# Lending one PSUM bank of the block products to the small products beside them

## The chip, the cores and the metric

The kernel runs on one core of a Trainium2 chip. The metric is the time of one execution on the device in microseconds, as the median of the runs. One execution is profiled, and the profile's "span" is the time from its first to its last recorded instruction. Engines are named as the profile names them: PE (matrix multiplies), PEld (its weight loads), DVE, ACT, POOL, and SP, which only issues transfers here.

## What is computed

One inference step of one layer, for 1024 prompt rows and for 8 samples of 4 rows, all with 1024 channels. After a normalisation the rows are multiplied by `w_in`, whose columns feed two branches and the gates:

```python
def layer(x, c, C0, n0, m0, k_past, v_past, ...):
    h, gate = adaln_in(x, c, w_ada, b_ada, g_norm)
    mq, mk, mv, mi, mf, mo, mz, aq, ak, av, az, gm, ga = split_in(h @ w_in)
    y_m, C, n, m = mlstm_branch(mq, mk, mv, mi, mf, mo, mz, C0, n0, m0, b_i, b_f, g_mn)
    ...
    o = attn_prompt(q, k, v, sinks)
    ...
    y_a = o.astype(x.dtype) * jax.nn.silu(az)
    u = jax.nn.sigmoid(gm) * (y_m @ w_mo) + jax.nn.sigmoid(ga) * (y_a @ w_ao)
    x = x + gate * (u @ w_o)
```

The mLSTM branch has 4 heads with a matrix memory that is carried over chunks of 128 rows. The attention branch has 8 query heads on 2 key heads, sees a window of 128 rows, and has a sink term in its softmax. Everything is float32. At the end stands another normalisation, and the memories, keys and values are outputs too.

## The kernel before

**Big products.** The large multiplications with `w_in` go in pairs of 128-column jobs over all 1024 prompt rows: 20 pairs, of the kinds `head_in` (6, the inputs of the mLSTM heads), `gate` (8), `query_gate` (2, the attention's output gate) and `head_gate` (4). `block_products` (L1511) does each pair by a scheme with 7 products instead of 8, numbered 1 to 7. Each is 12 matmuls of 128x512, since every operand is split into a high and a low part and three of the four combinations are summed. Sums and differences of blocks are formed beforehand, partly on DVE, partly by copying one product's bank into the next one's, from which it goes on accumulating. From the second pair on, the order is 5, 6, 2, 7, then product 1 of the next pair, then 3, 4. In the first pair product 5 stands ahead of 3.

**PSUM.** There are 8 banks, two for each of the tags g, a, b and o (L197 to 207). Product 1 takes a bank of g (`bx`, called X), which goes on into product 2; W (`bw`, from g) is a copy of X and goes into products 3 and 6. Tag a holds product 5 (`bz`, called Z, L1550) and Y (`by`, L1563), which starts as a copy of W and goes into products 7 and 4. Product 5 is copied out to SBUF by ACT, right behind the product in the program:

```python
                elif i == 5:
                    p5 = ht([128, 512], "p5")
                    S.copy(p5, Z)
```

The bank is not used again until product 5 of the next pair. Small products share the two b banks and the two o banks.

**Small products** come from generators in streams: attention units `unit(g, b0)` (L836, 16 of them; the text calls them unit (3,4) and the like), mLSTM heads `head(h)` (L1027), `sample_head(h)` (L1147), the sample rows of each pair (`smp`, L1360, and `smpo`, L1372) and others. At each `yield lag, banks` a generator says when its next visit is due and which banks that takes. In a unit the visits are: scores `sc` into one o and one b bank, which DVE reads together with the mask (the profile's `CUSTOM_DVE_ANT_0 p<-sc,cst,sink`) for the maximum; exponentials on ACT, and the load of V rows from `vdD` over the queries in `uqv`; the division; the transposes `pt` into a b bank; `oT`, the product with V, into a b bank.

**The planner.** `Side` (L115) decides at build time where small products go. It has a clock, `side.now`, that each matmul moves on by its estimated time, and `tick` is called after every third matmul of a big product. A visit is put in when it is due and its banks are free by the planner's account: a bank counts as taken for 3.5 us (b) or 5.5 us (o) after each use.

```python
HOLD = {"b": 3.5, "o": 5.5}
...
    def fits(self, banks):
        return all(sorted(self.free[b])[banks.count(b) - 1] <= self.now for b in set(banks) & set(HOLD))
```

PE's order is thereby fixed in the program. On DVE, ACT and SP a scheduler of the framework orders the instructions, and what a buffer or bank has to wait for is put in as semaphores. A PE instruction whose bank isn't free yet holds up all of PE behind it. A transfer that SP issues waits on SP for what it overwrites, and holds up the transfers behind it.

**Stages beside each other.** Units run first, beside pairs 1 to 7. Heads start when units are done (`side.held`): head 0 loads its inputs (`hq`, `hk`, `hkn`, `hv`, the exponents `et`, the weights `qw`) with six transfers on SP, and its first steps on DVE are `MEMSET hv`, `et<-et,cst` and `qw<-qw,hq`. Sample heads come among the later heads. When the last big product is done, everything left in the streams is put in, and then the output products `g_w_ao`, `g_w_mo` and the last product with `w_out` follow (banks `foX`, `foW`, `foZ`, `foY`).

Of the kernel before, what the change touches and what calls it, by code (L numbers as in the profile page):

```python
# [10 lines left out]
F32 = mybir.dt.float32  # L11
# [98 lines left out]
HOLD = {"b": 3.5, "o": 5.5}  # L110


class Side:
# [4 lines left out]
    def __init__(self, each, limits, quiet, patience):  # L118
        self.each, self.patience, self.free = each, patience, {b: [0.0, 0.0] for b in HOLD}
        self.now, self.last, self.quiet, self.products = 0.0, 0.0, quiet, 0  # L120
        self.held = {}
        self.streams = {n: {"max": m, "gap": g, "wait": [], "live": [], "next": 0.0} for n, (m, g) in limits.items()}

    def add(self, stream, gen, banks=""):
# [16 lines left out]
    def tick(self, joined=False):  # L141
        self.each()
        for name, st in self.streams.items():
            held = name in self.held and self.held[name]()
            if st["wait"] and not held and len(st["live"]) < st["max"] and self.now >= st["next"]:
                self.begin(st)
        ripe = sorted((i for st in self.streams.values() for i in st["live"] if self.now >= i[1]), key=lambda i: i[1])
        for item in [i for i in ripe if not i[2]]:
            self.step(item)
        ripe = [i for i in ripe if i[2] and self.now >= i[1]]  # L150
        able = [i for i in ripe if self.fits(i[2])]
        late = [i for i in able if self.now >= i[1] + self.patience]
        if not joined and (self.now < self.last + self.quiet or (len(able) < 2 and not late)):
            return
        kept = set()
        for item in sorted(ripe, key=lambda i: "r" in i[2] or -("t" in i[2])):
            if not self.fits(item[2]) or kept & set(item[2]):
                if self.now >= item[1] + self.patience:
                    kept |= set(item[2])
                continue  # L160
            self.take(item[2])
            self.step(item)
            self.last = self.now

    def fits(self, banks):
        return all(sorted(self.free[b])[banks.count(b) - 1] <= self.now for b in set(banks) & set(HOLD))

    def take(self, banks):
        for b in (b for b in banks if b in HOLD):
            self.free[b].remove(min(self.free[b]))  # L170
            self.free[b].append(self.now + HOLD[b])

    def until(self, done):
        while not done():
# [14 lines left out]
def body(tc, a):  # L189
    nc = tc.nc  # L190
    with ExitStack() as ctx:
        cp = ctx.enter_context(tc.tile_pool(name="cp", bufs=1))
        sp = ctx.enter_context(tc.tile_pool(name="sp", bufs=1))
        ps = ctx.enter_context(tc.tile_pool(name="ps", bufs=1, space=PSUM))
        dp = ctx.enter_context(tc.tile_pool(name="dp", bufs=1, space=DRAM))

        def pg(shape, name):  # L197
            return ps.tile(shape, F32, tag="g", bufs=2, name=name)

        def pa(shape, name):  # L200
            return ps.tile(shape, F32, tag="a", bufs=2, name=name)

        def pb(shape, name):
            return ps.tile(shape, F32, tag="b", bufs=2, name=name)

        def po(shape, name):
# [78 lines left out]
            free.append(ins)  # L285

        side = Side(stores, {"m": (2, 35.0), "a": (5, 7.0), "x": (2, 0.0), "s": (2, 20.0), "g": (1, 0.0), "e": (2, 0.0)}, 2.0, 4.0)
        def mm(out, lhsT, rhs, start, stop, share=1, more=False):
            n = int(np.prod(rhs.shape[1:]))
            side.now += max(n, 250) / 2400 if rhs.dtype == F32R else max(n * 4 // share, 128) / 2400  # L290
            side.products += 1
            in_order(nc.tensor.matmul(out, lhsT, rhs, start=start, stop=stop, skip_group_check=more))  # L292
# [171 lines left out]

        def x_rows(p, dg):
            n = PARTS[p][1]
            rows = (pa, pa, pg)[p]([128, 512], f"xb{p}")[:, :n]
            for c in range(0, n, 128):
                m = min(128, n - c)
                mm(rows[:, c:c + m], one[:m], dg[:m, c:c + m], start=True, stop=True)  # L470
            return rows
# [59 lines left out]
        banks = [pg]  # L531
# [979 lines left out]
        def block_products(jobs, hook):  # L1511
            flat = [(0, 1)]
            for n in range(len(jobs)):
                nx = [(n + 1, 1)] if n + 1 < len(jobs) else []
                flat += [(n, i) for i in (5, 6, 2, 7)] + nx if n else [(n, 6), (n, 2), (n, 7)] + nx + [(n, 5)]
                flat += [(n, 3), (n, 4)]

            def split_ahead(j):
                if j < len(flat):
                    jobs[flat[j][0]].split(flat[j][1])  # L1520

            bank = lambda pool, name: pool([128, 512], name)
            jobs[0].load()
            yield
            jobs[0].samples()
            split_ahead(0)
            jobs[0].first_sums()
            split_ahead(1)
            yield

            def filled(pool, name, src, n):
                b = bank(pool, name)
                if n == 0:
                    mm(b, wh[:, 0], blocks["b11"][0][0], start=True, stop=True)
                S.copy(b, src)
                return b

            X, W, Y, Z, NX = None, None, None, None, None
            for j, (n, i) in enumerate(flat):
                job_ = jobs[n]  # L1540
                nxt = jobs[n + 1] if n + 1 < len(jobs) else None
                hook(n, i)
                job_.kind.ahead(job_, i)
                if i == (5 if n else 1) and nxt:
                    nxt.load()
                split_ahead(j + 2)
                if i == 1:
                    o = NX = bank(pg, "bx")
                elif i == 5:
                    o = Z = bank(pa, "bz")  # L1550
                else:
                    o = {2: X, 3: W, 4: Y, 6: W, 7: Y}[i]
                new = i in (1, 5)
                wh, wl = job_.w.pop(i)
                for k in range(4):
                    bh, bl = blocks[OPERANDS[i]][k]
                    mm(o, wh[:, k], bh, start=(new and k == 0), stop=False, more=not new)
                    mm(o, wh[:, k], bl, start=False, stop=False, more=not new)
                    mm(o, wl[:, k], bh, start=False, stop=(k == 3), more=not new)
                    if k < 3:  # L1560
                        side.tick()
                if i == 6:
                    Y = filled(pa, "by", W, n)  # L1563
                elif i == 2:
                    job_.done(0, 0, X)
                elif i == 5:
                    p5 = ht([128, 512], "p5")
                    S.copy(p5, Z)
                elif i == 3:
                    job_.done(0, 1, p5, W)  # L1570
                elif i == 4:
                    job_.done(1, 0, Y)
                if i == (7 if n else 5):
                    job_.done(1, 1, p5, Y)
                if i == (2 if n else 7) and nxt:
                    nxt.samples()
                    nxt.first_sums()
                if j == 0 or (i == 3 and nxt):
                    X = NX
                    W = filled(pg, "bw", X, j)  # L1580
                side.tick()
# [46 lines left out]
        def first_split(n, i, eng):  # L1628
# [16 lines left out]
        rows = {p: x_rows(p, dgs[p]) for p in (0, 2)}  # L1645
# [12 lines left out]
        rows[1] = x_rows(1, dgs[1])  # L1658
        acc = [(pg([128, 384], "g_ak0"), po([128, 384], "g_av0")),
               (po([128, 384], "g_ak1"), pg([128, 384], "g_av1")),  # L1660
               (pa([128, 384], "g_ak2"), pa([128, 384], "g_av2"))]
        for q, kk in enumerate(two):
            more = q < len(two) - 1
            if q == 2:
# [143 lines left out]
            pass  # L1808
        side.until(lambda: not any(side.streams[n]["wait"] or side.streams[n]["live"] for n in "mase"))
        side.finish("x")  # L1810
        banks[:] = [pg, pg, pa, pa]
        ut = [quarter(x, [128, 4, T], "u") for x in ("h0", "h1")]
        u = lambda k, c0, n: ut[k // 4][:, k % 4, c0:c0 + n]
        ymt = [quarter(x, [128, 4, T], "ym", F32R) for x in ("l0", "l1")]
# [74 lines left out]
        rows = [quarter(x, [128, 4, D], "rows") for x in ("l0", "l1")]  # L1889
# [40 lines left out]
        v, e, y, w = (sm([128, 1], f"fl{i}", 1) for i in range(4))  # L1930
# [55 lines left out]
        def copied(src, name, pool=None, c=slice(0, 512), new=None):  # L1986
            t = ht([128, 512], name) if pool is None else pool([128, 512], name)[:, :c.stop - c.start]
            if new:
                mm(t, new.w[1][0][:, 0], wo["b11"][0][0][:, c], start=True, stop=True)
            S.copy(t, src[:, c])  # L1990
            return t
# [4 lines left out]
        xb = ss = None  # L1996
        for i, r in enumerate(blocks_of_rows):
# [1 line left out]
            aside = lambda *when: next(rows8, None) if i in when else None  # L1999
            before, xb, ss = (xb, ss), [residual(2 * i + c) for c in range(2)], sm([128, 6], "fss", 2)  # L2000
            aside(0)
            X, Z = pg([128, 512], "foX"), pa([128, 512], "foZ")
            r.product(1, X, True)
            W = copied(X, "foW", pg, new=r if i == 0 else None)
            if i:
# [12 lines left out]
            aside(1)  # L2018
            r.product(6, W, False)
            parts = ((0, 512),) if nxt else ((0, 256), (256, 256))  # L2020
            Y = [copied(W, f"foY{c0}", pb if c0 else pa, slice(c0, c0 + n), r if c0 or i == 0 else None) for c0, n in parts]
            r.start(4)
            out_split(1)
            aside(2)
# [124 lines left out]
```

## Time and profile before

| | |
|---|---|
| Median of 3 runs | 816.17 us (815.36 to 816.26) |
| The profiled execution | 816.73 us |
| Its span | 814.9 us |
| Granted PE clock, mean | 0.998 |
| PE busy | 795.6 us |
| DVE busy | 601.2 us |
| ACT busy | 409.2 us |
| POOL busy | 105.3 us |

What lies between the span and the profiled execution's time (1.8 us) is outside the recorded instructions. A row of a timeline has the start and the duration of an instruction, both in us, then engine, line, operation, and output and inputs; in brackets stands how long the engine had been idle and what ended that. Matmuls overlap: their starts, not their durations, give the pace. The program's names carry numbers that tell buffers apart; the timeline leaves most of them out. The windows view has for each stretch its length, then the busy time of PE, PEld, DVE, ACT and POOL, the granted clock, the share of the transfer engines, and GB/s.

### The profile page before, as it was taken

The page shows a single profiled execution, that of the slowest core. Times are in us where ns is not written, and L with a number is a line of the kernel's source. Part 1 is how long each engine was busy: PE and PEld are TensorE (multiplying, and loading weights), DVE is VectorE, ACT ScalarE, POOL GpSimd, SP SyncE. Part 2 cuts the span into 40 slices and gives each one's busy share as a digit, 9 for nine tenths or more (in the row PEclk, how much of TensorE's full clock was granted, in tenths as well). Part 3 has the DMA queues.
Part 4 walks back from the last instruction along what each step waited for, and adds up shares of the span by engine and source line. Part 5 has one row for each costly group of instructions (what it writes and reads, how often), then busy time and mean ns, then how long its engine had stood idle before and what let it go on. Part 6 is the DMA issues. An engine that isn't in the chain of part 4 may idle for free.

```text
span 814.9 us, 15087 instructions
## 1 busy us (share of the span) xinstructions
PE 795.6 (98%) x5071; PEld 650.3 (80%) x5071; DVE 601.2 (74%) x1631; ACT 409.2 (50%) x996; POOL 105.3 (13%) x196
## 2 busy tenths in 40 slices
PE   6899999999999999999999999999999999999996
PEld 2688887777777767887888888787788999997785
DVE  3789747989776866665766787899786677767576
ACT  4674243655646757645454655564545244215344
POOL 0220000222222220010211110111101100000041
PEclk9999999999999999999999999999999999999999
DMA  9977646878785475744364675573455698534532
GB/s 322 373 228 203 177 125 223 265 228 238 249 249 168 115 220 171 226 135 150 101 184 133 184 188 172 160 210 91 138 169 185 227 346 305 173 102 167 204 110 104
DMA packets 111041, 157.26 MB, mean 193 GB/s; under 512 B 19712, under 2 KB 61440, under 8 KB 110932
## 3 DMA queue, kind: packets, MB, share of 16 engines
q1 hardware_dynamic: 96148, 135.58, 52.5%
q10 hardware_dynamic: 11232, 14.42, 5.0%
q0 software_dynamic: 3584, 6.30, 3.9%
q8 instruction: 40, 0.66, 0.4%
q14 instruction: 37, 0.30, 0.1%
HBM read 112.58 MB, written 44.69 MB: 193 GB/s over the span
## 4 chain that ended last, share of the span: by engine, by line
PE 93%; DVE 2%; DMA 2%; ACT 1%; issue 1%; SPq 0%; ACTq 0%; DVEq 0%
PE bw L292 14%; PE by L292 13%; PE bx L292 13%; PE bz L292 7%; PE g_aq L292 6%; PE g_w_mo L292 6%; PE g_w_ao L292 5%; PE foX L292 3%; PE foW L292 2%; PE smp L292 2%; PE foY L292 2%; PE sc L292 2%; PE oT L292 2%; PE n L292 2%; PE g_ak L292 1%; PE g_av L292 1%
## 5 line engine op out<-in xcount | busy, mean ns | idle before, releaser
L273 POOL DMA_DIRECT2D yhD<-yt x48 | 28.8, 607 | 230.9 <-DVE yt L235 139.6
L292 PE MATMUL g_w_ao<-ya,wh_w_ao 128*128 128x384 f32 (+1 forms) x192 | 45.7, 322 | 0.1
L292 PE MATMUL g_w_mo<-ym_l,wh_w_mo 128*128 128x384 f32 (+1 forms) x192 | 45.7, 323 | 0.0
L235 ACT ACTIVATE p<-p,nmx 128x256 f32<-128x256 f32 (+1 forms) x64 | 31.0, 486 | 21.4 <-DVE nmx L235 20.7
L273 POOL DMA_DIRECT2D mkN<-mkt x32 | 20.9, 659 | 133.5 <-DVE p L235 71.8
L292 PEld LDWEIGHTS g_w_ao<-ya,wh_w_ao 128*128 128x128 f32 x192 | 33.5, 188 | 0.7 <-DVE ya L235 0.6
L292 PEld LDWEIGHTS g_w_mo<-ym_l,wh_w_mo 128*128 128x128 f32 x192 | 33.5, 188 | 0.0
L292 PE MATMUL g_aq<-h_h,wh_aq 128*128 128x384 f32 (+1 forms) x96 | 31.9, 333 | 0.0
L292 PE MATMUL g_aq<-h_l,wh_aq 128*128 128x384 f32 (+1 forms) x96 | 31.0, 323 | 0.0
L292 PE MATMUL g_w_mo<-ym_l,wl_w_mo 128*128 128x384 f32 (+1 forms) x96 | 31.0, 323 | 0.0
L292 PE MATMUL g_aq<-h_h,wl_aq 128*128 128x384 f32 (+1 forms) x96 | 31.0, 323 | 0.0
L292 PE MATMUL g_w_ao<-ya,wl_w_ao 128*128 128x384 f32 (+1 forms) x96 | 30.8, 321 | 0.0
L235 ACT CAST uwh<-u_h 128x512 fp32r<-128x512 f32 x27 | 16.6, 620 | 27.3 <-PE foY L292 10.5
L235 DVE TENSOR_TENSOR uwl<-u_h,uwh 128x512 fp32r<-128x512 f32 x27 | 18.5, 689 | 12.5 <-ACT uwh L235 12.4
L235 DVE CUSTOM_DVE_ANT_0 p<-sc,cst,sink 128x256 f32<-128x256 f32 (+1 forms) x64 | 26.1, 461 | 1.0 <-PE sc L292 1.0
L273 POOL DMA_DIRECT2D mvN<-mvt x32 | 20.7, 653 | 37.3 <-DVE mvt L235 36.3
L235 ACT CAST wo_h<-wo_l 128x512 fp32r<-128x512 f32 x28 | 17.1, 620 | 13.8 <-DVE u_h L235 10.6
L235 POOL TENSOR_TENSOR fr_w<-fr_y 128x2 f32<-128x2 f32 (+1 forms) x12 | 3.5, 291 | 144.2 <-DVE fr_y L235 143.6
L235 ACT ACTIVATE p<-p,den 128x128 f32<-128x128 f32 x56 | 18.6, 394 | 5.1 <-DVE den L235 4.5
L235 DVE TENSOR_TENSOR wo_l<-wo_l,wo_h 128x512 fp32r<-128x512 f32 x28 | 18.7, 686 | 2.5 <-ACT wo_h L235 2.4
L235 DVE SCALAR_TENSOR_TENSOR p<-p,den 128x128 f32<-128x128 f32 x56 | 17.3, 345 | 4.2 <-ACT wh_pgate__3658 L235 2.9
L292 PEld LDWEIGHTS g_aq<-h_h,wh_aq 128*128 128x128 f32 x96 | 18.0, 188 | 2.7 <-issue 2.5
(1621 smaller groups left out, 2684.3 us busy)
## 6 DMA issues: line engine op xcount, KB each, us to landing
x<-xT SPq DMA_DIRECT2D x16, 256.0 KB
early_h<-w_ada SPq DMA_DIRECT2D x8, 512.0 KB
adar_ga<-w_ada SPq DMA_DIRECT2D x16, 256.0 KB
ow<-w_out SPq DMA_DIRECT2D x16, 256.0 KB
woD_t<-ow SPq DMA_DIRECT2D x16, 256.0 KB
wr_ga<-w SPq DMA_DIRECT2D x16, 256.0 KB
wr_gm<-w SPq DMA_DIRECT2D x16, 256.0 KB
taD<-gt ACTq DMA_DIRECT2D x16, 256.0 KB
```

What stands on the lines that cost most here:

```text
L235: ins = f(*args, **kw)
L273: nc.gpsimd.dma_start(out, in_)
L292: in_order(nc.tensor.matmul(out, lhsT, rhs, start=start, stop=stop, skip_group_check=more))
```

## The change

Tag a is split into two tags of one bank each: z for product 5 (and, outside the block products, for `xb0`, `g_ak2`, `foZ`), y for Y (and `xb1`, `g_av2`, `foY`). After each product 5 the planner is told that bank z may be lent from 1.5 us after the product until 3.5 us before the next product 5, which is six big products later (two in the first pair). Within that time a visit that needs a b bank gets z whenever it is open, also when a b bank is free; `pb` then allocates from z. One tile at a time is lent: each loan closes the bank for 3.5 us.

```diff
+    def open(self):
+        return self.spare <= self.now <= self.until_
+
+    def lend(self, start, end):
+        self.spare, self.until_ = start, end - HOLD["b"]
+
     def fits(self, banks):
-        return all(sorted(self.free[b])[banks.count(b) - 1] <= self.now for b in set(banks) & set(HOLD))
+        return all((b == "b" and self.open()) or sorted(self.free[b])[banks.count(b) - 1] <= self.now
+                   for b in set(banks) & set(HOLD))
 
     def take(self, banks):
+        self.grant = "b" in banks and self.open()
         for b in (b for b in banks if b in HOLD):
-            self.free[b].remove(min(self.free[b]))
-            self.free[b].append(self.now + HOLD[b])
+            if b == "b" and self.grant:
+                self.spare = self.now + HOLD[b]
+            else:
+                self.free[b].remove(min(self.free[b]))
+                self.free[b].append(self.now + HOLD[b])
+
+    def granted(self):
+        g, self.grant = self.grant, False
+        return g
...
-        def pa(shape, name):
-            return ps.tile(shape, F32, tag="a", bufs=2, name=name)
+        def pz(shape, name):
+            return ps.tile(shape, F32, tag="z", bufs=1, name=name)
+
+        def py(shape, name):
+            return ps.tile(shape, F32, tag="y", bufs=1, name=name)
...
         def pb(shape, name):
+            if at_side and at_side[0].granted():
+                return pz(shape, name)
             return ps.tile(shape, F32, tag="b", bufs=2, name=name)
...
                 elif i == 5:
-                    o = Z = bank(pa, "bz")
+                    o = Z = bank(pz, "bz")
...
                 if i == 6:
-                    Y = filled(pa, "by", W, n)
+                    Y = filled(py, "by", W, n)
...
                     S.copy(p5, Z)
+                    after = [i for _, i in flat[j + 1:]]
+                    gap = (after + [5]).index(5)
+                    side.lend(side.now + 1.5, side.now + gap * 12 * 512 / 2400)
```

The planner's `tick` also clears the grant after each visit; the remaining lines rename `pa` to `pz` or `py` where it was used. The instructions of every engine are the same in number and kind. What moves is the place of small products among the big ones, and with it the order on the other engines. Three places show it, all around the score product `sc` of attention unit (3,4) (its names end in `sc_4_0` and `sc_4_1`, for the two key heads) and the start of head 0.

PE, before: the scores stand behind the sample products `smp` of a gate pair, ahead of its `by` product.

```order
L292 MATMUL smp<-wr_gm_0_3439,c_106 32x128
L292 MATMUL smp<-wr_gm_1_3441,c_106 32x128
L292 MATMUL sc_4_0_3599<-ukv,uqv 128x256
L292 MATMUL sc_4_1_3600<-ukv,uqv 128x256
L292 MATMUL sc_4_0_3599<-ukv,uqv 128x256
L292 MATMUL sc_4_1_3600<-ukv,uqv 128x256
L292 MATMUL by<-t3h_911,wh_pgate_7__3489 128x512
L292 MATMUL by<-t3l_912,wh_pgate_7__3489 128x512
L292 MATMUL by<-t3h_911,wl_pgate_7__3490 128x512
```

PE, after: they stand behind the `oT` of unit (2,6), ahead of the `bx` product that those sample products follow.

```order
L318 MATMUL oT_6_3536<-p_3229,uqv 64x128 x2
L318 MATMUL oT_6_3536<-p_3230,uqv 64x128 x2
L318 MATMUL oT_6_3536<-p_3229,uqv 64x128 x2
L318 MATMUL sc_4_0_3549<-ukv,uqv 128x256
L318 MATMUL sc_4_1_3550<-ukv,uqv 128x256
L318 MATMUL sc_4_0_3549<-ukv,uqv 128x256
L318 MATMUL sc_4_1_3550<-ukv,uqv 128x256
L318 MATMUL bx<-h_h_584,wh_pgate_2__3459 128x512
L318 MATMUL bx<-h_l_585,wh_pgate_2__3459 128x512
L318 MATMUL bx<-h_h_584,wl_pgate_2__3460 128x512
```

The scores have moved up by one big product and the `smp` interlude behind it.

SP, before, at the loads of head 0 (`hq0_0` to `qw`); `uqv<-vdD` are the loads of V rows, of units (3,2), (3,4) and (3,6) in turn, `uqv<-qD` and `ukv<-kD` the queries and keys of unit (3,6):

```order
L277 DMA uqv_3260<-vdD_111 128x512
L277 DMA uqv_3510<-qD_112 128x256
L277 DMA ukv_3511<-kD_110 128x384
L277 DMA hq0_0_3547<-qD0_134 128x384
L277 DMA hk0_0_3548<-kD0_135 128x384
L277 DMA hkn0_0_3549<-mkN0_142 128x3x128
L277 DMA hv0_0_3550<-mvN0_146 128x3x128
L277 DMA et_3555<-nmd_1484 128x384
L277 DMA qw_3556<-wid_1485 128x384
L277 DMA uqv_3431<-vdD_111 128x512
L277 DMA uqv_3510<-vdD_111 128x512
```

SP, after, at the same place; the load of V rows into `uqv_3399` is that of unit (3,4):

```order
L301 DMA uqv_3511<-qD_112 128x256
L301 DMA ukv_3512<-kD_110 128x384
L301 DMA uqv_3399<-vdD_111 128x512
L301 DMA hq0_0_3570<-qD0_134 128x384
L301 DMA hk0_0_3571<-kD0_135 128x384
L301 DMA hkn0_0_3572<-mkN0_142 128x3x128
L301 DMA hv0_0_3573<-mvN0_146 128x3x128
L301 DMA et_3578<-nmd_1484 128x384
L301 DMA qw_3579<-wid_1485 128x384
L301 DMA uqv_3511<-vdD_111 128x512
```

The V load of the unit whose scores moved up now stands ahead of head 0's six transfers, and that of unit (3,2) still further up, out of these rows.

DVE, before, from head 0's `MEMSET hv` to the first read of unit (3,4)'s scores, the `ISA` row at the end:

```order
L235 TENSOR_TENSOR p_3332<-pt_0_3524,cst 128x512
L235 MEMSET hv_0_3550 128x3
L235 SCALAR_TENSOR_TENSOR p_3458<-p_3458,den 128x128 x2
L235 SCALAR_TENSOR_TENSOR p_3458<-p_3459,den 128x128
L235 TENSOR_TENSOR et<-et,cst 128x384
L235 SCALAR_TENSOR_TENSOR p_3458<-p_3459,den 128x128
L235 TENSOR_TENSOR wl_pgate_3__3618<-wr_ga_1_3085,wh_pgate_3__3617 128x512
L235 TENSOR_TENSOR wl_pgate_4__3659<-wr_gm_1_3089,wh_pgate_4__3658 128x512
L235 TENSOR_TENSOR wr_gm_0_3439<-wr_ga_0_3435,wr_gm_0_3439 128x512
L235 TENSOR_TENSOR qw<-qw,hq_0_3547 128x384
L235 TENSOR_TENSOR wr_ga_0_3435<-ws_3612,wr_ga_0_3435 128x512
L235 ISA p_3596,mx<-sc_4_0_3599,cst,sink 128x256
```

DVE, after: the `ISA` row at the start is the last read of the same scores, and head 0's `et` and `qw` come at the end, with `MEMSET hv` two rows further on.

```order
L259 ISA p_3547,mx<-sc_4_1_3550,cst,sink 128x256
L259 ISA mx 128x1
L259 TENSOR_SCALAR nmx<-mx 128x4
L259 TENSOR_TENSOR nmx<-sink,mx 128x4
L259 TENSOR_TENSOR den<-den,nmx 128x4
L259 TENSOR_TENSOR wr_gm_0_3455<-wr_ga_0_3451,wr_gm_0_3455 128x512
L259 RECIPROCAL den<-den 128x4
L259 TENSOR_TENSOR wl_pgate_4__3690<-wr_gm_1_3089,wh_pgate_4__3689 128x512
L259 TENSOR_TENSOR wr_ga_0_3451<-ws_3634,wr_ga_0_3451 128x512
L259 TENSOR_TENSOR p_3428<-pt_2_3627,cst 128x512
L259 TENSOR_TENSOR et<-et,cst 128x384
L259 TENSOR_TENSOR qw<-qw,hq_0_3570 128x384
```

The reads of unit (3,4)'s scores have passed head 0's first steps.

More of the change, by code (lines that the diff above doesn't have):

```diff
@@ L121, in __init__ @@
         self.held = {}
+        self.spare, self.until_, self.grant = 0.0, -1.0, False
         self.streams = {n: {"max": m, "gap": g, "wait": [], "live": [], "next": 0.0} for n, (m, g) in limits.items()}
@@ L162, in tick @@
             self.step(item)
+            self.grant = False
             self.last = self.now
+    def open(self):
+        return self.spare <= self.now <= self.until_
+    def lend(self, start, end):
+        self.spare, self.until_ = start, end - HOLD["b"]
     def fits(self, banks):
-        return all(sorted(self.free[b])[banks.count(b) - 1] <= self.now for b in set(banks) & set(HOLD))
+        return all((b == "b" and self.open()) or sorted(self.free[b])[banks.count(b) - 1] <= self.now
+                   for b in set(banks) & set(HOLD))
     def take(self, banks):
+        self.grant = "b" in banks and self.open()
         for b in (b for b in banks if b in HOLD):
-            self.free[b].remove(min(self.free[b]))
-            self.free[b].append(self.now + HOLD[b])
+            if b == "b" and self.grant:
[6 more added lines that the diff above has]
+        return g
     def until(self, done):
@@ L198, in pg @@
             return ps.tile(shape, F32, tag="g", bufs=2, name=name)
-        def pa(shape, name):
-            return ps.tile(shape, F32, tag="a", bufs=2, name=name)
+        def pz(shape, name):
+            return ps.tile(shape, F32, tag="z", bufs=1, name=name)
+        def py(shape, name):
+            return ps.tile(shape, F32, tag="y", bufs=1, name=name)
+        at_side = []
         def pb(shape, name):
+            if at_side and at_side[0].granted():
+                return pz(shape, name)
             return ps.tile(shape, F32, tag="b", bufs=2, name=name)
@@ L287, in body @@
         side = Side(stores, {"m": (2, 35.0), "a": (5, 7.0), "x": (2, 0.0), "s": (2, 20.0), "g": (1, 0.0), "e": (2, 0.0)}, 2.0, 4.0)
+        at_side.append(side)
         def mm(out, lhsT, rhs, start, stop, share=1, more=False):
@@ L466, in x_rows @@
             n = PARTS[p][1]
-            rows = (pa, pa, pg)[p]([128, 512], f"xb{p}")[:, :n]
+            rows = (pz, py, pg)[p]([128, 512], f"xb{p}")[:, :n]
             for c in range(0, n, 128):
@@ L1660, in body @@
                (po([128, 384], "g_ak1"), pg([128, 384], "g_av1")),
-               (pa([128, 384], "g_ak2"), pa([128, 384], "g_av2"))]
+               (pz([128, 384], "g_ak2"), py([128, 384], "g_av2"))]
         for q, kk in enumerate(two):
@@ L1810, in body @@
         side.finish("x")
-        banks[:] = [pg, pg, pa, pa]
+        banks[:] = [pg, pg, pz, py]
         ut = [quarter(x, [128, 4, T], "u") for x in ("h0", "h1")]
@@ L2001, in body @@
             aside(0)
-            X, Z = pg([128, 512], "foX"), pa([128, 512], "foZ")
+            X, Z = pg([128, 512], "foX"), pz([128, 512], "foZ")
             r.product(1, X, True)
@@ L2020, in body @@
             parts = ((0, 512),) if nxt else ((0, 256), (256, 256))
-            Y = [copied(W, f"foY{c0}", pb if c0 else pa, slice(c0, c0 + n), r if c0 or i == 0 else None) for c0, n in parts]
+            Y = [copied(W, f"foY{c0}", pb if c0 else py, slice(c0, c0 + n), r if c0 or i == 0 else None) for c0, n in parts]
             r.start(4)
```

## The prediction

> **What bounds the kernel now.** I read the page first (engine shares and the chain that ended last), then the windows and the waits of PE for the part in which the change acts, then the timeline around the waits that were left.
>
> From the page of before:
>
> ```profile
> span 814.9 us, 15087 instructions
> PE 795.6 (98%) x5071; PEld 650.3 (80%) x5071; DVE 601.2 (74%) x1631; ACT 409.2 (50%) x996; POOL 105.3 (13%) x196
> PE 93%; DVE 2%; DMA 2%; ACT 1%; issue 1%; SPq 0%; ACTq 0%; DVEq 0%
> ```
>
> PE is busy for 98% of the span and carries 93% of the chain. The change adds and removes no matmul, so it can only win back PE's idle time. The windows view shows how much of that there is, in the stretch with the block products and the small products beside them (PE's column is the second):
>
> ```profile
> 260.00:310.00 50.00, 47.74 (x338) 36.09 (x338) 35.51 (x114) 33.98 (x108) 10.33 (x16) 1.00 0.57 171
> 310.00:632.00 322.00, 321.90 (x2092) 261.63 (x2091) 240.74 (x730) 172.06 (x431) 34.06 (x57) 1.00 0.55 164
> ```
>
> From 310 to 632 us PE idles 0.10 us, and from 260 to 310 us 2.26 us, at a granted clock of 1.00. The waits view of PE between 110 and 640 us has two rows:
>
> ```profile
> PE pt L297 <- DVE mx L235: 2.3, 1, 2.3
> PE bw L292 <- ACT bw L235: 0.7, 1, 0.7
> ```
>
> The second is a wait for a copy into bank W, which the change doesn't touch. The first is a wait for a PSUM bank. PE's timeline around it:
>
> ```profile
> 295.32 0.40 PE L292 MATMUL bx<-h_h,wh_pgate__3443 128*128 128x512 f32 x1
> ...
> 299.20 1.13 PE L292 MATMUL sc<-ukv,uqv 64*128 64x256 f32 x8
> ...
> 303.21 0.88 PE L292 MATMUL oT<-p,uqv 128*64 128x128 f32 x12
> 306.35 0.66 PE L297 MATMUL pt<-cst,p 128*128 128x128 f32 x4 [2.26 <-DVE mx L235]
> ```
>
> The transposes `pt` of attention unit (3,2) need a bank of tag b. One holds the tile `oT` just written, the other the scores `sc` of unit (3,4), which PE had finished at 300.33. DVE's timeline says why they lay there for six microseconds:
>
> ```profile
> 299.05 0.35 DVE L235 SCALAR_TENSOR_TENSOR p<-p,den 128x128 f32<-128x128 f32 x1 [2.93 <-ACT wh_pgate__3658 L235]
> ...
> 300.98 0.56 DVE L235 TENSOR_TENSOR et<-et,cst 128x384 f32<-128x384 f32 x1 [1.06 <-DMA et<-nmd]
> ...
> 304.60 0.48 DVE L235 CUSTOM_DVE_ANT_0 p<-sc,cst,sink 128x256 f32<-128x256 f32 x1
> ...
> 305.81 0.48 DVE L235 CUSTOM_DVE_ANT_0 p<-sc,cst,sink 128x256 f32<-128x256 f32 x1
> ```
>
> The readers of `sc` stand in DVE's row behind the first steps of head 0 (`et` among them). DVE idled 2.93 us ahead of them and 1.06 us for the load of `et`; the last read ended at 306.29, and `pt` began 0.06 later. So all that a third bank for small products can win here is 2.26 us, 0.28% of the span.
>
> **The change part by part.** *Own homes.* Products 5 and by already took turns on the two banks of tag a; with a tag each they lie as before: nothing, in either direction.
>
> *The loan.* Following the planner's clock through the program, 33 small tiles go to bank z. Until planned time 223 no instruction moves on any engine; only the bank differs. There a lent tile must wait until ACT has copied product 5 out of z, which the planner takes to be done 1.5 us after the product. Before, only the next pair's product 5 waited for that copy. The closest case is the `oT` of unit (1,4). PE, and ACT beside it:
>
> ```profile
> 234.78 0.39 PE L292 MATMUL bz<-h_h,wl_phead_in__2701 128*128 128x512 f32 x1
> ...
> 237.19 0.98 PE L292 MATMUL oT<-p,uqv 128*64 128x128 f32 x14
> ```
>
> ```profile
> 237.33 0.58 ACT L235 COPY p<-bz 128x512 f32<-128x512 f32 x1
> ```
>
> The product ended at 235.17, its copy at 237.91, and `oT` wants to start at 237.19. PE is in order, so the whole of 0.72 us and a hand-over (0.06 above) stands still: 0.8 us. The other lent tiles of this first part start after their copies have ended. Bounds: 0, if ACT takes the copy ahead of its cast in the new run, and 1.2, if it comes one ACT instruction of this size (0.58) later. I take 0.8, since ACT's row is unmoved there.
>
> *The moved scores.* From planned time 223 on, attention visits go earlier. `sc` of unit (3,4) now stands before the `bx` product that began at 295.32, four microseconds ahead of its place at 299.20, and in z. Its reads stand ahead of head 0's steps on DVE. The bank that `pt` waited for is then free, and the 2.26 us go. What is late next is on SP, whose timeline before is:
>
> ```profile
> 292.55 1.79 SPq L277 DMA_DIRECT2D hq<-qD  x1
> ...
> 295.40 0.44 SPq L277 DMA_DIRECT2D hv<-mvN  x1
> 295.89 0.53 SPq L277 DMA_DIRECT2D et<-nmd  x1
> ...
> 300.40 0.32 SPq L277 DMA_DIRECT2D uqv<-vdD  x1
> ```
>
> The last row is the load of unit (3,4)'s V rows over its queries, issued 0.07 after `sc` ended at 300.33. In the changed order this load stands ahead of `hq`, and it still waits for `sc`: 295.3 and 1.13 make 296.4, with the interlude's start some 0.3 more. So `hq` to `et` are queued behind a waiting DMA. The five issues ahead of `et`'s own (0.4 to 0.5 each) take 2.3 us, and `et` goes out at about 299.0 instead of 295.89. It took 5.1 us to be there (300.98 less 295.89), so it lands at about 304.1, up to 0.5 later if `hq` issues slowly again. DVE now comes to `et` at about 303.5 with everything ahead of it done, and waits 0.6 to 1.1. Behind that wait stand the score reads of unit (3,6), which I place at an end of 309.9. The next user of their bank, `oT` of unit (3,2), comes up on PE at about 310.2 (both are estimates, by laying the changed order over the rows above). The slack is 0.3 us: a new wait of 0 (which I take, since the two estimates leave it) to 1.5 (if `hq` stalls as it did, 1.79 less 0.4).
>
> *Interludes.* Small products between large ones cost PE two changes of shape. PE's timeline around one:
>
> ```profile
> 601.76 0.40 PE L292 MATMUL bx<-h_h,wl_phead_gate__7160 128*128 128x512 f32 x1
> 602.09 0.30 PE L292 MATMUL smp<-wr_mo,c 128*32 128x128 f32 x2
> ...
> 603.41 0.41 PE L292 MATMUL st<-sz,cst 128*32 128x129 f32 x2
> 603.75 0.50 PE L292 MATMUL by<-t3h,wh_phead_gate__7191 128*128 128x512 f32 x1
> 604.09 0.40 PE L292 MATMUL by<-t3l,wh_phead_gate__7191 128*128 128x512 f32 x1
> 604.33 0.39 PE L292 MATMUL by<-t3h,wl_phead_gate__7192 128*128 128x512 f32 x1
> ```
>
> Large products start 0.24 apart (604.09 to 604.33); into the interlude it is 0.33, and after the first large one behind it 0.34. That is 0.2 us for each interlude. The orders have 82 of them before and 83 now, with the same small products: +0.2.
>
> *Later steps.* The four heads end about 10 us later by the planner's clock, and the last two visits of the last sample head now stand behind the last large product, just ahead of `g_w_ao`. Their input is ready: in before the scaling that feeds them followed the `st` of 603.41 thus:
>
> ```profile
> 609.23 0.33 DVE L235 TENSOR_SCALAR sz<-sz,fsden,fsr_y 32x128 f32<-32x128 f32 x1
> ```
>
> From 603.41 to 609.56 are 6.2 us, and five large products (12 times 0.23 each, 13.8 us) lie between the two steps in the changed order. Those products are their cover; without it PE would wait up to 6.2. I cost it at nothing.
>
> The sum on the profiled execution: 816.73 - 2.26 + 0.8 + 0.2 = 815.47. That execution was 0.56 above the median of the runs shown (816.17), so the forecast is 814.9.
>
> The idle row bears on one rule. PE's 2.26 us were spent for want of a bank. The Trainium skill, page "Perfetto Trace Analysis", section "Matmul Optimizations", asks that all eight PSUM banks be used, for parallelism between instructions. By it the loan is pure gain, which would be 814.1, the rival "only gain" below. Against it stand the 0.10 us in 322 from 310 us on, where two b banks sufficed.
>
> **The rivals.**
>
> *A wait in place of the one removed, no gain.* The load of V ahead of head 0's loads delays `et` so far that `oT` of (3,2) waits 1.5 us, or the `pt` wait stays in another guise. For it: `et` already held DVE for 1.06. Against: in the new order the critical reads stand ahead of `et`. Sum with the new wait 1.5: -2.26 + 0.8 + 0.2 + 1.5 = +0.2, so 816.4; with the whole wait kept: +1.0, so 817.2. The Trainium skill, page "TensorE: Matmul & The Clock Gate", section "HAM oscillation — how this bites in real kernels", tells of a kernel whose PE had been made dense and to which a doubling of PSUM buffers then gave no further gain (126.6 us and 125.5). By that rule too it would be this case; the trace bears it out everywhere but at 306 us.
>
> *Only gain.* ACT's copy comes in time for `oT` of (1,4), and the interlude is free: -2.26 + 0.2 is -2.1, so 814.1. For it: the copy is late by one cast of 0.61 only. Against: that ACT row has no move in it.
>
> *Slower: the copy of product 5 late in the sample heads.* Today a copy out of z may be late at no cost, and some are:
>
> ```profile
> 573.61 0.39 PE L292 MATMUL bz<-h_h,wl_phead_gate__6790 128*128 128x512 f32 x1
> 578.84 0.57 ACT L235 COPY p<-bz 128x512 f32<-128x512 f32 x1
> ```
>
> This copy ended 5.4 us after its product (579.41 less 574.00), behind casts of the sample head on ACT. In the changed program lent tiles of sample heads come 3.7 and 3.3 us after product 5 of the pairs before the last two (by the planned clock). With such a copy in both places PE stands 1.7 and 2.1 us: -2.26 + 0.8 + 0.2 + 3.8 = +2.5, so 818.7; with one of them +0.4 to +0.8. It decides when a copy ends more than 3.3 us after its product. Against: in the changed ACT order one instruction or none stands between the product's step and its copy there.
>
> That the change does nothing can be ruled out for the order (rows have moved), though not for the time, which is the first rival.
>
> **How the numbers follow.** The chances: forecast 0.43 (own range 814.3 to 815.6: the `oT` wait between 0.2 and 1.2 moves it by -0.6 and +0.4, and a late `et` may add 0.3), no gain 0.24 (816.4 to 817.2), only gain 0.15 (813.6 to 814.5), slower 0.18 (816.6 to 818.7). The forecast's 814.9 is the likeliest. From 813.6 to 818.0 lie the first three and a quarter of the last, 0.86 less what each may miss by; the three runs of before lay within 0.9 of each other. A measurement can tell about 0.2% from no change, 1.63 us: faster is below 814.5, slower above 817.8. Faster: most of "only gain" (0.13) and a quarter of the forecast (0.11), 0.24. Slower: four fifths of the last case (0.14) and the edge of "no gain" (0.04), 0.18. The rest, 0.58, is the same.
>
> **What would show it.** In the trace after: no row `pt <- DVE mx` in PE's waits, and PE's busy time in a window like 260 to 310 near 50; a new row of `oT` waiting about 0.8 us for ACT near 237 us; `hq` on SP behind `uqv<-vdD`, with `et` some 3 us later. Wrong: a wait of `oT` or `pt` on DVE between 300 and 312 (first rival); a lent `sU`, `st` or `sty` waiting for ACT's copy from bz after 500 us (last rival); a change of PE's busy time, or of idle time outside 110 to 640 us, which I hold still.

## The result, and the profile after

The changed kernel takes 822.70 us (median of 6 runs, 821.62 to 825.55), the kernel before, in runs beside it, 815.92 us (median of 6, 814.80 to 816.42). The ratio is 1.0091, with a 95% interval of 1.0073 to 1.0108 (the two medians alone make 1.0083): slower by 6.8 us, where 1.3 us less had been forecast, and above the upper end of the range.

The profiled execution of the changed kernel, from its page:

```profile
span 820.5 us, 15110 instructions
PE 797.2 (97%) x5071; PEld 651.8 (79%) x5071; DVE 601.8 (73%) x1631; ACT 408.9 (50%) x996; POOL 104.9 (13%) x196
PE 89%; DMA 5%; DVE 3%; ACT 1%; issue 1%; SPq 0%; ACTq 0%; DVEq 0%
```

The span is 5.6 us longer, PE is busy 1.6 us longer with the same 5071 instructions, and 5% of the chain that ended last now lies in transfers, where it was 2%. PE's waits between 110 and 640 us, after:

```profile
PE bx L318 <- DVE zt L259: 4.7, 1, 4.7
PE bw L318 <- ACT bw L259: 1.0, 2, 0.7
PE bx L318 <- ACT gt L259: 0.5, 1, 0.5
```

The wait of `pt` is gone, and there is a new one twice its size. The windows view, first for the place of the old wait, then around the new one (the figure behind POOL's column is the granted clock):

```profile
260.00:310.00 50.00, 49.98 (x360) 37.68 (x360) 39.49 (x130) 34.44 (x109) 10.29 (x16) 1.00 0.64 192
```

```profile
502.00:507.00 5.00, 0.58 (x3) 0.15 (x1) 3.10 (x8) 2.25 (x7) 0.00 (x0) 1.00 0.61 205
507.00:514.00 7.00, 6.73 (x18) 4.85 (x19) 3.90 (x17) 1.64 (x7) 0.00 (x0) 0.52 0.29 80
```

PE stands for 4.7 us, and for the next 7 us it is granted a clock of 0.52: it looks busy and does half the work, which costs another 7 times 0.48, 3.4 us. In PE's timeline the large matmuls that started 0.23 apart start 0.43 apart:

```profile
501.96 0.39 PE L318 MATMUL by<-t3l,wh_pquery_gate__5811 128*128 128x512 f32 x1
502.19 0.39 PE L318 MATMUL by<-t3h,wl_pquery_gate__5812 128*128 128x512 f32 x1
507.27 0.79 PE L318 MATMUL bx<-h_h,wh_pquery_gate__5859 128*128 128x512 f32 x1 [4.69 <-DVE zt L259]
507.86 0.63 PE L318 MATMUL bx<-h_l,wh_pquery_gate__5859 128*128 128x512 f32 x1
508.29 0.63 PE L318 MATMUL bx<-h_h,wl_pquery_gate__5860 128*128 128x512 f32 x1
```

This `bx` is product 1 of the second `query_gate` pair. Its bank of tag g held X of the first such pair, which ACT and DVE turn into a tile `zt` (`silu_of`). The chain that ended last shows for this stretch what that waited for (start, length, what):

```profile
494.42 6.25 DMA qw<-wid
...
500.73 5.14 DMA C_s<-Cs
...
505.90 0.60 ACT zt L259
...
507.27 1.65 PE bx L318 x3
```

`C_s<-Cs` is the store of sample head 0's state. `zt` comes from the same pool of 49 SBUF buffers (`half`, `ht` in the code) as the state tile `Cs`, and was given that tile's buffer, so ACT could not write it before the store had read it. SP issued the store only at 500.73, though DVE's last step on the tile ended at 497.62: in the built program a semaphore holds the store until the eighth transfer ahead of it on SP has landed, and that was the load of `qw` for head 2 (issued at 494.42, landed at 500.67). In the kernel before, the same store and the same first `zt` (SP, then ACT):

```profile
485.95 3.18 SPq L277 DMA_DIRECT2D C_s<-Cs  x2
```

```profile
501.40 0.59 ACT L235 ACTIVATE zt<-bx 128x512 f32<-128x512 f32 x1
```

There the store went out 15.5 us ahead of `zt`, and the two do not share a buffer: by the addresses in the built programs, `zt` follows a tile `gt` in its buffer there, and the buffer of the state goes to the copy of a product 5, which ACT writes 9.9 us after the store's issue:

```profile
495.89 0.58 ACT L235 COPY p<-bz 128x512 f32<-128x512 f32 x1
```

In the changed plan the first step on that state comes 13.0 us later (DVE's `Cs` at 496.00 instead of 483.03), PE is through with this X 2.7 us earlier than before, and the pool, dealt out in another order, gives `zt` the state's buffer.

The sum over the profiled executions, up to the first `g_w_ao` (in before, then after):

```profile
632.08 0.51 PE L292 MATMUL g_w_ao<-ya,wh_w_ao 128*128 128x384 f32 x2
```

```profile
638.21 0.42 PE L318 MATMUL g_w_ao<-ya,wh_w_ao 128*128 128x384 f32 x1
```

That is 6.1 us later: -2.26 for `pt`, +4.69 for `zt`, +3.4 for the clock, +0.3 and +0.5 for the two small waits make +6.6, and 0.5 stays unassigned.

### The profile page after: what moved, and what is told of

Same layout as the page of the kernel before. It is cut to its first block, busy times and chain, and to the rows that moved or that the text cites. A ratio compares the mean times of both kernels' runs of the same rounds, so it can differ in the third digit from the quotient of the medians.

```text
span 820.5 us, 15110 instructions
## 1 busy us (share of the span) xinstructions
PE 797.2 (97%) x5071; PEld 651.8 (79%) x5071; DVE 601.8 (73%) x1631; ACT 408.9 (50%) x996; POOL 104.9 (13%) x196
## 4 chain that ended last, share of the span: by engine, by line
PE 89%; DMA 5%; DVE 3%; ACT 1%; issue 1%; SPq 0%; ACTq 0%; DVEq 0%
PE bx L318 13%; PE bw L318 13%; PE by L318 12%; PE g_aq L318 6%; PE bz L318 6%; PE g_w_mo L318 6%; PE g_w_ao L318 6%; PE foX L318 3%; PE foW L318 2%; PE smp L318 2%; PE foY L318 2%; PE sc L318 2%; PE oT L318 2%; PE n L318 2%; PE g_ak L318 1%; PE g_av L318 1%
## 5 line engine op out<-in xcount | busy, mean ns | idle before, releaser
L259 DVE TENSOR_TENSOR h_l<-x,h_h 128x512 fp32r<-128x512 f32 x20 | 13.7, 692 | 7.2 <-ACT h_h L259 5.9
```

The lines of the kernel that those rows point to most:

```text
L259: ins = f(*args, **kw)
```

## The experiments

For all of them the ratio is to runs of the kernel before on the same chip (medians 816.74, 816.22 and 815.79 us on the three occasions).

**1. Homes only.** The tags are split, nothing is lent.

```diff
-                    side.lend(side.now + 1.5, side.now + gap * 12 * 512 / 2400)
+                    gap = 0
```

> Product 5 and by have their own tags z and y, and nothing is lent; every engine's order is that of before. Theory (the loan's new plan puts sample head 0's store of its state late, the first zt tile of the first query_gate pair gets that store's SBUF buffer, PE waits 4.7 us for it and then runs on half the clock): nothing of this happens, so the time of before, 815.9 (within 0.1%). Rival (the split of tag a itself costs something): above 817.

Measured: 815.67 us, ratio 0.9993 (0.9978 to 1.0009). No cost of the split shows. In this execution the old wait is there, but shorter, though every engine's order is that of before:

```profile
PE pt L323 <- DVE mx L259: 1.2, 1, 1.2
```

So the 2.26 us of the profiled execution were not a constant. DVE's two idle stretches ahead of the late reads were 2.19 and 0.70 here, 2.93 and 1.06 in before, which is the same 1.1 us.

**2. The bank without a re-plan.** `fits` is that of before, and `take` books a b bank as before, also where `pb` then gives out z.

```diff
-        return all((b == "b" and self.open()) or sorted(self.free[b])[banks.count(b) - 1] <= self.now
-                   for b in set(banks) & set(HOLD))
+        return all(sorted(self.free[b])[banks.count(b) - 1] <= self.now for b in set(banks) & set(HOLD))
...
                 self.spare = self.now + HOLD[b]
-            else:
-                self.free[b].remove(min(self.free[b]))
-                self.free[b].append(self.now + HOLD[b])
+            self.free[b].remove(min(self.free[b]))
+            self.free[b].append(self.now + HOLD[b])
```

> The planner decides as in before, and only pb gives out bank z when it is open: PE's and SP's orders are those of before, and small tiles lie in three banks. Theory (the re-planning is what costs, the bank is a gain): the wait of pt at 306 us goes and the zt wait at 502 us does not come, 815.9 - 2.3 = 813.7 (813.3 to 814.5). Rival (small tiles in bank z wait for, or hold up, product 5): new waits of PE for the copy from bz, as slow as after or at least no faster than before, 816 to 822.

Measured: 816.97 us, ratio 1.0009 (0.9991 to 1.0026): neither. PE's waits:

```profile
PE bw L316 <- ACT bw L257: 1.1, 2, 0.7
PE smpo L316 <- DVE p L257: 1.1, 1, 1.1
```

The re-plan is needed for the loss, as the theory said. But the gain it expected fails: `pt` found its bank, and 5 us later `smpo` waited 1.1 for a bank that the same late DVE had not read. The third bank passed the wait on.

**3. Another buffer for zt.** The changed kernel; the first `zt` tile is taken from the pool at product 5 and handed to `silu_of` later.

```diff
+        early = []
...
-            t = ht([128, 512], name)
+            t = early.pop() if name == "zt" and early else ht([128, 512], name)
...
                     c, th = {5: (0, 0), 6: (1, 1), 2: (0, 1), 7: (1, 0)}[i]
+                    if i == 5 and self.i == 0:
+                        early.append(ht([128, 512], "zt"))
+                        G.memset(early[0][:, 0:1], 0.0)
```

> The changed kernel, with PE's order unmoved; the first zt tile is taken from the pool one product earlier (a one-element memset on POOL claims it), so that it gets another SBUF buffer than the one which the store of sample head 0's state is still reading. Theory: the 4.7 us wait of PE and the half clock behind it (some 3 us) both go, 822.7 - 7.8 = about 815, between 814 and 816.5. Rival (DVE and ACT are late there in any case, since heads and sample heads crowd): the wait stays within 1 us or comes back as another, 820 to 823.

Measured: 816.81 us, ratio 1.0003 (0.9991 to 1.0015). PE's waits:

```profile
PE by L318 <- DVE ztz L259: 0.9, 1, 0.9
PE oT L318 <- ACT p L259: 0.7, 1, 0.7
PE bw L318 <- ACT bw L259: 0.7, 1, 0.7
PE bx L318 <- ACT hg L259: 0.5, 1, 0.5
```

ACT now writes `zt` before SP has even issued the store:

```profile
497.87 0.59 ACT L259 ACTIVATE zt<-bx 128x512 f32<-128x512 f32 x1
```

```profile
498.05 0.70 SPq L301 DMA_DIRECT2D C_s<-Cs  x1
```

With one buffer exchanged the 4.7 us and the half clock are gone, and the ratio falls from 1.0091 to that of no change. The median is 0.3 above the expected band, the kernel before being 0.8 higher than on the first occasion, and the 2.3 us of `pt` are not won in the balance: other small waits are there, among them `oT`'s wait for product 5's copy, 0.7, which the prediction had put at 0.8.

**4. Loans among the units only.**

```diff
-                    side.lend(side.now + 1.5, side.now + gap * 12 * 512 / 2400)
+                    if len(units_done) < 16:
+                        side.lend(side.now + 1.5, side.now + gap * 12 * 512 / 2400)
```

> The changed kernel, lending only as long as attention units are unfinished; PE's order is that of the changed kernel up to its 2622nd instruction, beyond the wait at 502 us. Theory (the loans among the units move the heads, and that alone leads to the late store): as slow as the changed kernel, 821 to 824. Rival (the loans to head and sample-head tiles cost the time): near before or faster, 813.5 to 816.5.

Measured: 823.76 us, ratio 1.0089 (1.0070 to 1.0107), with the same wait:

```profile
PE bx L318 <- DVE zt L259: 4.6, 1, 4.6
```

Loans made while units run (PE is through with the last of them at 328 us) suffice for a wait at 502 us; no tile of a head or sample head has to lie in z.

**5. The store from another queue.** The changed kernel, with the stores of the sample heads' states issued by POOL.

```diff
-                store(a["C_s"][h][:, 4 * i:4 * i + 4], c)
+                scatter(a["C_s"][h][:, 4 * i:4 * i + 4], c)
```

> The changed kernel, with PE's order unmoved; the stores of the sample heads' states are issued by POOL at once instead of by SP behind head 3's loads. Theory (the late store is what the first zt tile waits for): the first store goes out when DVE is done with the state, about 497.7 instead of 500.7, and is there 2.5 to 5 us later; PE's wait of 4.7 shrinks to 0 to 1.7 and the half clock behind it goes: 822.7 - 3.7 - 3.3 = 815.7, between 814 and 817. Rival (ACT or DVE are late there for other reasons): above 819.

Measured: 820.82 us, ratio 1.0055 (1.0037 to 1.0073). POOL issues the store with DVE's last step, but ACT still waits for it (POOL, ACT, and PE's waits):

```profile
496.76 0.58 POOL L297 DMA_DIRECT2D C_s<-Cs  x1 [5.44 <-DVE Cs L259]
```

```profile
503.97 0.60 ACT L259 ACTIVATE zt<-bx 128x512 f32<-128x512 f32 x1 [1.17 <-DMA C_s<-Cs]
```

```profile
PE bx L318 <- DVE zt L259: 3.9, 1, 3.9
```

The expectation fails on the transfer's length: it took until 503.97, 7.2 us, where 2.5 to 5 had been set. Issuing it early shortens the wait by less than a microsecond. What makes the transfer slow was not taken apart; the loads of head 3 go at the same time, and from 497 to 500 us the transfer engines were busy 0.97 of the time.

**6. The heads' first steps on POOL, in the kernel before.** No loan, two b banks.

```diff
-                V.tensor_tensor(et[:, :m], et[:, :m], cmask.unsqueeze(1).to_broadcast((128, m, 128)), op=ALU.add)
-                V.tensor_tensor(qw[:, :m], qw[:, :m], q[:, :m * 128].rearrange("p (c e) -> p c e", e=128), op=ALU.mult)
+                G.tensor_tensor(et[:, :m], et[:, :m], cmask.unsqueeze(1).to_broadcast((128, m, 128)), op=ALU.add)
+                G.tensor_tensor(qw[:, :m], qw[:, :m], q[:, :m * 128].rearrange("p (c e) -> p c e", e=128), op=ALU.mult)
...
-                V.memset(vn[:, :m, 128:129], 1.0)
+                G.memset(vn[:, :m, 128:129], 1.0)
```

> The kernel before, with the first steps of the heads' inputs (the et sum, the qw product and the memset into hv) on POOL instead of DVE; two b banks, no loan, PE's order unmoved. Theory (the wait at 306 us came from DVE's queue, which stood behind head 0's loads, and the bank only passed it on): the pt wait goes without a third bank, ratio 0.997 to 0.9985 to before. Rival (two banks are too few there): pt still waits 1 us or more, ratio 0.9995 to 1.001.

Measured: 814.13 us, ratio 0.9970 (0.9958 to 0.9983). One wait is left to PE between 110 and 640 us:

```profile
PE bw L292 <- ACT bw L235: 0.7, 1, 0.7
```

The wait at 306 us needed no bank: it was gone once DVE no longer stood behind head 0's loads. On another occasion:

> The kernel before with the heads' first steps on POOL once more, on another occasion. Theory (the 306 us wait came from DVE's queue): again a ratio of 0.996 to 0.9985. Rival (the first measurement was luck of the chip): 0.9985 to 1.001.

Measured: 814.41 us, ratio 0.9983 (0.9973 to 0.9994). The sign holds, the size is 1.4 to 2.4 us by the two ratios. This is the version that beats both kernels.

**7. The same steps on POOL in the changed kernel.**

> The changed kernel with the same three steps on POOL. Theory (the zt wait comes from SP's late store and the reused buffer, not from DVE's load): zt still waits 4 us or more, 820 to 823. Rival (DVE's crowding by heads and sample heads makes it late): the wait falls under 2 us, 814 to 817.

Measured: 824.76 us, ratio 1.0095 (1.0072 to 1.0118):

```profile
PE bx L318 <- DVE zt L259: 4.4, 1, 4.4
PE bx L318 <- ACT gt L259: 1.6, 1, 1.6
PE oT L318 <- ACT p L259: 1.6, 1, 1.6
PE bw L318 <- ACT bw L259: 1.3, 2, 0.7
```

It is even above the expected band. `zt` still comes late, as the theory said, but the store isn't what held it last here. ACT did not idle ahead of `zt`; it came to it behind steps on `et`, which had waited for POOL and so for a load. The chain that ended last:

```profile
501.41 5.88 DMA et<-nmd
...
507.43 0.87 POOL et L259
...
509.30 0.49 ACT zt L259
```

The store had gone out at 503.81; how long it alone would have held `zt` isn't shown. So this run says only that relieving DVE doesn't free `zt`; that the store and the buffer hold it rests on the other experiments.

**8. The steps on POOL and the bank without a re-plan** (the edits of 2 and 6).

> Heads' first steps on POOL, and bank z lent without a re-plan (PE's order that of before). Theory (once DVE's queue is cured, PE has no wait left that a bank could end): the same as prep_again within 0.1%, 0 to 1 us slower where a lent tile waits for product 5's copy. Rival (a third bank is worth something of its own): 1 us or more faster than prep_again.

Measured: 814.25 us, ratio 0.9988 (0.9976 to 1.0000), against 814.41 beside it. The third bank adds nothing to 6.

**9. Both cures in the changed kernel** (the edits of 3 and 6).

> The changed kernel with the re-planned loan, with both cures: the heads' first steps on POOL and the first zt tile taken early. Theory (zt's wait and the half clock behind it were the whole loss; what is left are small waits of oT and gt for ACT, together up to 3 us as in the run with the steps on POOL alone): the zt wait is gone, 815 to 818. Rival (the re-plan is bad in itself): 820 or more.

Measured: 819.78 us, ratio 1.0047 (1.0031 to 1.0063). It misses both bands:

```profile
PE by L318 <- DVE fsv L259: 2.3, 1, 2.3
PE bw L318 <- ACT bw L259: 1.8, 2, 1.2
PE bx L318 <- ACT gt L259: 1.5, 1, 1.5
```

`zt`'s wait is gone, but three others sum to 5.6, with a spell of half clock behind the longest. So the re-planned order is also worse in places other than `zt`; why these waits grow when head steps go to POOL was not taken apart.

**10. A re-plan without a loan.** The kernel before, with one number of the planner changed, first down (hold30), then up (hold40).

```diff
-HOLD = {"b": 3.5, "o": 5.5}
+HOLD = {"b": 3.0, "o": 5.5}
```

> The kernel before without any loan, but the planner takes a b bank as held for 3.0 instead of 3.5 us, which moves small products from the units on. Theory (any re-plan deals the waits behind it anew, since the planner sees neither SBUF buffers nor SP's queue): the time differs from before, with another set of waits in PE's list; I expect a ratio outside 0.999 to 1.001, on either side. Rival (only the loan costs): ratio within 0.999 to 1.001 and the same two waits as before.

Measured: 823.09 us, ratio 1.0084 (1.0056 to 1.0112), with waits of small products for DVE (at 306 us) and ACT (at 193 us), which had not yet read the banks, since tiles are packed closer:

```profile
PE smp L292 <- DVE mx L235: 2.7, 1, 2.7
PE sc L292 <- ACT ukv L235: 2.1, 1, 2.1
```

```diff
-HOLD = {"b": 3.5, "o": 5.5}
+HOLD = {"b": 4.0, "o": 5.5}
```

> The kernel before without a loan; the planner takes a b bank as held for 4.0 instead of 3.5 us, another re-plan. Theory (each re-plan deals a new set of waits): PE's list of waits differs from that of before; the ratio is outside 0.998 to 1.002, more likely slower. Rival (only shorter holds or a loan, which pack tiles closer, cost time): within 0.999 to 1.002, no wait above 2 us.

Measured: 824.09 us, ratio 1.0105 (1.0088 to 1.0122). PE's longest wait, and the chain that ended last in that stretch:

```profile
PE bx L292 <- DVE zt L235: 3.6, 1, 3.6
```

```profile
495.26 6.82 DMA qw<-wid
...
502.15 4.68 DMA C_s<-Cs
506.83 0.02 issue
506.85 0.60 ACT zt L235
```

There is no loan and no third bank here, and the same store holds the same `zt`: this plan too gives it the state's buffer. What costs in both is a plan that brings sample head 0's store close to the first `query_gate` product and lets `zt` follow in its buffer. In the run with 3.0 it was other waits.

## Why the prediction was wrong

- **What bounds the kernel, and that at most 2.26 us could be won:** right about where PE idled. But the term was one execution's (1.2 in experiment 1), and its cause was DVE's place behind head 0's loads, which the prediction had named and then treated as a matter of banks. Experiments 2, 6 and 8 show it: a bank alone 1.0009, the steps off DVE 0.9970 and 0.9983, both 0.9988. The Trainium skill's rule on using all eight PSUM banks (page "Perfetto Trace Analysis", section "Matmul Optimizations") gave the rival "only gain"; here the banks were all in use in some form, and lending one out was worth nothing.
- **Own homes at nothing:** right (0.9993).
- **The copy of product 5 at 0.8:** right as a mechanism, and luck in size. In the profiled execution of after it was 0: ACT took the copy at 234.98, 2.3 us earlier than in before, as DVE had been ahead. In two other runs of the same PE order (experiments 3 and 7) it was 0.7 and 1.6, the second beyond the bound of 1.2.
- **The interlude at 0.2:** not told apart by any run; the sum above leaves 0.5 unassigned.
- **The moved scores and SP's queue:** right. `et` was taken at 303.99, after a wait of 0.51 for its load (304.1 and 0.6 to 1.1 had been worked out), and no wait of PE came of it:

```profile
298.78 0.42 SPq L301 DMA_DIRECT2D et<-nmd  x1
```

```profile
303.99 0.56 DVE L259 TENSOR_TENSOR et<-et,cst 128x384 f32<-128x384 f32 x1 [0.51 <-DMA et<-nmd]
```

- **"Later steps" at nothing: this step failed.** "The four heads end about 10 us later by the planner's clock" was followed only to the end of the large products, where its cover of 13.8 us held: no wait of `sty` or `smpo` came. It was not followed to what else the late sample heads hold: SBUF buffers of a shared pool, until SP's stores have read them. The step that was costed at nothing measured 4.7 us and the half clock behind it, 3.4. What the trace of before could show was the room: from the store's issue to the next write into that buffer 9.9 us, from which a transfer of some 5 leaves 5, less than the delay of 10 (the store went out 14.8 us later in the end). Which tile would follow in the buffer could be read only from the changed program. Experiments 3, 4 and hold40 show the cause.
- **The rivals:** the slower side was given 0.18, for late copies of product 5 with sample heads' tiles in z. No such wait came. The right side was there for a wrong reason.
- **The price of a wait:** costed one for one throughout. The long one took 4.7 and then 3.4 more, and PE's busy time, which was to hold still, rose by 1.6 us net.

## What to carry to other kernels

When a change lets a planner decide anew, the moved work carries its buffers, loads and stores with it: for each group that moves, put the distance between its last store and the next user of that buffer in the old trace beside the distance by which it moves. A new plan also deals the pool's buffers anew, so read from the new program which tile follows in the buffer, and what holds the store on its queue. In a kernel whose PE waits twice in 500 us, a re-plan of any kind has little to win and many tight spots to find; three different ones cost 0.8 to 1.1% here. Ask of a wait for a bank why the bank isn't read: moving the reader's neighbours cured what a third bank only passed on.

## What the runs showed of the hardware

After a long wait PE was granted half its clock, for 3.4 us or two or three times that. It was 3.4 us after waits of 2.3 (experiment 9), 2.7 (hold30, at 306 us) and 3.9 (experiment 5), 6.8 after 3.6 (hold40), 4.6 (experiment 4) and 4.7 (the changed kernel), and 10.2 after 4.4 (experiment 7). So the length of the wait doesn't by itself set the length of the spell. Nor do the two start together: the clock fell 2.2 us into the wait in experiment 7, and 1.5 us after its end in hold30. These are windows of experiment 5 and of hold30:

```profile
507.00:509.00 2.00, 2.00 (x7) 1.71 (x7) 1.27 (x8) 0.76 (x4) 0.00 (x0) 0.50 0.72 181
```

```profile
308.00:310.00 2.00, 2.00 (x6) 1.61 (x5) 1.27 (x4) 1.50 (x7) 0.00 (x0) 0.50 0.35 131
```

After the 2.26 us of before it stayed at 1.00, and so it did after hold30's 2.1 at 193 us, but after the 2.3 us of experiment 9 it fell:

```profile
515.00:517.00 2.00, 2.00 (x11) 1.95 (x10) 1.93 (x9) 0.06 (x1) 0.00 (x0) 0.53 0.19 72
```

The Trainium skill (page "TensorE: Matmul & The Clock Gate", section "HAM oscillation — how this bites in real kernels") says that gaps of PE above some 3.4 us bring the clock down. The waits of 3.6 us and more agree; single waits of 2.7 and 2.3 us did it below that figure, so no sharp length can be read from these runs.
